# Issuing the one-hot sums of the expert keys one step behind their operands, loading stored activations and gates earlier, and pacing a gather's rest in a two-block transformer kernel

## The chip, the cores and the metric

The kernel runs on one core of one Trainium2 chip. The metric is the device time of one execution in microseconds (us). The core has five engines with instruction streams of their own: PE (TensorE, the matrix products), DVE (VectorE), ACT (ScalarE), POOL (GpSimd) and SP (SyncE, which here only issues transfers). 16 DMA engines do the transfers of all of them.

## The reference, cut to what matters

Two transformer blocks on 512 tokens of width 1024, in float32. The first has a convolution, sliding-window attention and a feed-forward part; the second has a gated mixing part, attention over selected keys, and, as its last part, a mixture of 16384 tiny experts, each a row of `u_tab` and a row of `v_tab`. The change lies in that last part alone:

```python
def peer(xn, wq, subkeys, u_tab, v_tab):
    q = (xn @ wq).reshape(bsz, s, PEER_HEADS, 2, PEER_HALF)
    sub = jnp.einsum('bshpd,hpnd->bshpn', q, subkeys)
    s_top, i_top = lax.top_k(sub, PEER_TOPK)
    cand = (s_top[..., 0, :, None] + s_top[..., 1, None, :]).reshape(...)
    cand_idx = (i_top[..., 0, :, None] * N_KEYS + i_top[..., 1, None, :]).reshape(...)
    best, pos = lax.top_k(cand, PEER_TOPK)
    expert = jnp.take_along_axis(cand_idx, pos, axis=-1)
    gate = jax.nn.softmax(best, axis=-1)
    ...
        a = jax.nn.gelu(jnp.einsum('td,ted->te', xb, u_tab[eb]))
        return jnp.einsum('te,ted->td', (gb * a).astype(vb.dtype), v_tab[eb])
```

Each token has 8 heads, 128 keys a half and 16 experts a head: 128 experts a token.

## The kernel before, in words

Products are made in float32 from a high and a low half of each factor, three matmuls for one (`mm3`, L155 to L158). Weights stream through `unit` (L132 to L141) in pieces of 128x1024, 512 KB: SP issues the load of `raw` (L134, four buffers), ACT rounds it to `whi` (L138), DVE subtracts for `wlo` (L140, four buffers each), PE uses both. PE can so be served up to four units ahead of what it computes, and DVE's `wlo` is the step that sets how far.

The expert part takes two ways. Tokens 0 to 319 go through **all** experts as dense products: activations of 320 tokens with every row of `u_tab`, times a gate matrix G that is zero but for the chosen experts, times `v_tab`. Tokens 320 to 511 (half a block of 128 and the whole last block) fetch their experts' rows from memory instead: `gathered` (L950 to L968) lets POOL fetch 128 rows a time (L944, seven buffers `rows`), and DVE multiplies and adds them: 64 times for the half block (L952), 128 times for the last block with `u_tab` (L960), 128 times with `v_tab` (L967).

**The u stage** (about 1040 to 1470 us of the profile): 128 units of `u_tab`, of which 100 are computed here (`u_block`, L932 to L940, 24 matmuls 128x320 each), and their results are stored in memory (`a_dram`, 640 KB for four units). After each, the loop at L1189 to L1197 hands a budget of `R_US` = 3.6 us to a generator, `routed`, whose `yield`s say what they cost of it; a second generator, `gathered`, gets a share of it. What a generator issues before its budget is gone stands in the program behind that u-block. `routed` (L1150 and on) makes the gates for the blocks of 128 tokens in the order tb 2, 3, 0, 1:

- `keys` finds the 16 best sums, and then turns the positions of the best into key numbers in four steps (two halves of the pair, eight of 16 places each): DVE compares (L1033) and multiplies by a copy of the numbers (L1034) into `ohl` (two buffers), and PE adds up over the eight places by matmuls with a unit matrix (L1037, for tb 2 L1039 too). Then the gates are normalised and transposed on PE (L1067).
- `build` makes G of a block of tokens in 16 half-steps: DVE makes one-hot tiles `oh1`, `oh2` (L1097, L1098) and weighted ones `ohh`, `ohl` (L1104), PE multiplies them (L1111, 16 matmuls 128x128), ACT copies the sums out (L1112), and a whole step goes to memory (`g_dram`, L1117). The last eight half-steps of tb 2, the last of all, use three weighted tiles (`ohm` too, of which there is one buffer): five DVE instructions and 24 matmuls.
- Before those, the rest of the half block's gather is run off in one go (`while not made2: next(gat)`), and `weights2` turns its sums into gates.

**The v stage** (about 1470 to 2106 us): for each pair of units, `first` has the stored activations `al` of four units loaded (L1214, two buffers) or computes the pair's activations, `second` has the gates `gl` of eight units loaded (L1228, 1536 KB, two buffers) and multiplies them on DVE (L1231); the result is split (ACT `wvhi` L152, DVE `wvlo` L153), and two `v_block`s use it, 18 matmuls 128x512 each. 28 u-blocks that were not stored lie between. The gather for the last block runs beside it, a share for each v-block. SP issues its loads in the order of the program: an `al` whose buffer is not free yet holds up the `raw`s behind it.

A scheduler sets the order of DVE, ACT and SP instructions within what the program's order allows; the gather's DVE instructions are tied to stand behind the newest `wlo`.

## Time and profile before

| | us |
|---|---|
| runs | 2113.63, 2115.81, 2117.98 (median 2115.81) |
| profiled execution: its time, its span | 2110.99, 2109.3 |
| PE busy | 2050.9 (97%), 11120 matmuls |
| DVE busy | 1573.4 (75%) |
| ACT busy | 826.6 (39%) |
| POOL busy | 527.7 (25%) |
| mean granted TensorE clock | 0.992 of 2.4 GHz |

The span goes from the first instruction to the last one. The share of busy time is taken over the whole program; how PE and DVE stand to each other differs from stage to stage, so the rows below are mostly of single stretches. A line is that of the kernel before; the same instruction has a higher line number in the changed one (L1037 becomes L1030, L1104 becomes L1119, L1214 becomes L1225, L1228 becomes L1235, L1231 becomes L1259).

### The profile page before, as it was taken

What the parts mean: (1) busy time and instruction counts of PE and PEld (TensorE: products, weight loads), DVE (VectorE), ACT (ScalarE), POOL (GpSimd) and SP (SyncE); (2) the same over time, 40 slices, a digit from 0 to 9 for tenths busy, and PEclk for the clock granted to TensorE, in tenths of its full rate; (3) what the DMA queues carried; (4) which work ended last, traced back from release to release, by engine and by line L of the source; (5) the groups of instructions that cost most, each with busy time, mean ns of one, the idle gap of its engine ahead of it and who ended that gap; (6) DMA issues with size and microseconds to landing.
All of it is one profiled execution on the core that took longest, in us unless ns stands there. A gap on an engine that the chain in (4) does not pass through costs nothing.

```text
span 2109.3 us, 29516 instructions
## 1 busy us (share of the span) xinstructions
PE 2050.9 (97%) x11120; PEld 1747.3 (83%) x11120; DVE 1573.4 (75%) x2885; ACT 826.6 (39%) x1339; POOL 527.7 (25%) x383
## 2 busy tenths in 40 slices
PE   7999999999999999999989999999999999999999
PEld 6747888888887777888889899999888878788887
DVE  6984633332279954455699999998898888899997
ACT  5364432231254242333453455555333333233332
POOL 1000100000010000000032212220676666566673
PEclk9999999999999999999999999999999999999999
DMA  5202233333223212342288899999999999999996
GB/s 190 80 30 80 85 96 100 99 92 119 81 86 94 82 59 81 109 135 86 90 305 268 290 316 335 309 369 294 397 404 412 387 408 388 410 400 410 411 400 248
DMA packets 163281, 476.47 MB, mean 226 GB/s; under 512 B 13865, under 2 KB 57265, under 8 KB 161218
## 3 DMA queue, kind: packets, MB, share of 16 engines
q1 hardware_dynamic: 67104, 259.70, 35.1%
q0 software_dynamic: 46656, 169.18, 21.0%
q10 hardware_dynamic: 49378, 45.71, 6.5%
q8 instruction: 87, 1.43, 0.3%
q14 instruction: 56, 0.46, 0.1%
HBM read 432.18 MB, written 42.09 MB: 225 GB/s over the span
## 4 chain that ended last, share of the span: by engine, by line
PE 62%; DVE 17%; issue 12%; DMA 5%; POOL 2%; ACT 2%; DVEq 0%; POOLq 0%; SPq 0%; ACTq 0%; another core or an unknown queue 0%
PE bank_a L156 14%; PE bank_a L157 14%; PE bank_a L158 14%; PE bank_b L156 5%; PE bank_b L157 5%; PE bank_b L158 5%; DVE wlo L140 4%; DMA rows<-in_peer_u_dram,gidx 2%; DMA al<-a_dram 2%; POOL rows L944 2%; DVE rows L952 2%; DVE rows L960 2%; PE bank_b L1111 1%; DVE mask L710 1%; DMA rows<-in_peer_v_dram,gidx 1%
## 5 line engine op out<-in xcount | busy, mean ns | idle before, releaser
L138 ACT CAST whi<-raw 128x1024 fp32r<-128x1024 f32 (+1 forms) x413 | 431.9, 1047 | 879.1 <-PE bank_a L157 336.2
L140 DVE TENSOR_TENSOR wlo<-raw,whi 128x1024 fp32r<-128x1024 f32 (+1 forms) x413 | 499.9, 1213 | 264.1 <-ACT whi L138 261.7
L156 PE MATMUL bank_a<-xhi,whi 128*128 128x320 f32 (+2 forms) x1600 | 550.0, 345 | 0.8 <-ACT xhi L152 0.8
L158 PE MATMUL bank_a<-xhi,wlo 128*128 128x320 f32 (+2 forms) x1600 | 545.5, 341 | 3.7 <-DVE wlo L140 3.7
L157 PE MATMUL bank_a<-xlo,whi 128*128 128x320 f32 (+2 forms) x1600 | 546.7, 342 | 0.6 <-DVE xlo L153 0.6
L944 POOL DMA_INDIRECT rows<-in_peer_u_dram,gidx x192 | 284.1, 1480 | 546.3 <-DVE gidx L1045 144.4
L158 PEld LDWEIGHTS bank_a<-xhi,wlo 128*128 128x128 f32 x1600 | 302.9, 189 | 31.5 <-DVE wlo L140 5.7
L156 PEld LDWEIGHTS bank_a<-xhi,whi 128*128 128x128 f32 x1600 | 302.1, 189 | 29.3 <-issue 2.3
L157 PEld LDWEIGHTS bank_a<-xlo,whi 128*128 128x128 f32 x1600 | 303.0, 189 | 27.4 <-DVE xlo L153 1.6
L944 POOL DMA_INDIRECT rows<-in_peer_v_dram,gidx x128 | 207.1, 1618 | 114.6 <-DVE h L967 89.9
L156 PE MATMUL bank_a<-whi,wvhi 128*128 128x512 f32 x512 | 201.6, 394 | 6.4 <-ACT wvhi L152 6.4
L158 PE MATMUL bank_a<-whi,wvlo 128*128 128x512 f32 x512 | 200.8, 392 | 1.5 <-DVE wvlo L153 1.5
L157 PE MATMUL bank_a<-wlo,wvhi 128*128 128x512 f32 x512 | 201.4, 393 | 0.6 <-DVE wlo L140 0.6
L967 DVE SCALAR_TENSOR_TENSOR h<-rows,ga,h 128x1024 f32<-128x1024 f32 x128 | 164.2, 1282 | 5.9 <-DMA rows<-in_peer_v_dram,gidx 4.6
L173 POOL TENSOR_TENSOR rstd<-rstd,neghalf 128x1 f32<-128x1 f32 x20 | 13.9, 695 | 616.2 <-DVE rstd L172 616.2
L960 DVE SCALAR_TENSOR_TENSOR rows<-rows,h 128x1024 f32<-128x1024 f32 x128 | 152.6, 1217 | 8.1 <-DMA rows<-in_peer_u_dram,gidx 8.1
L156 PEld LDWEIGHTS bank_a<-whi,wvhi 128*128 128x128 f32 x512 | 96.8, 189 | 27.1 <-ACT wvhi L152 7.6
L158 PEld LDWEIGHTS bank_a<-whi,wvlo 128*128 128x128 f32 x512 | 96.9, 189 | 24.5 <-DVE wvlo L153 3.9
L157 PEld LDWEIGHTS bank_a<-wlo,wvhi 128*128 128x128 f32 x512 | 96.9, 189 | 20.5 <-DVE wlo L140 1.4
L157 PE MATMUL bank_b<-wlo,wvhi 128*128 128x512 f32 x256 | 99.6, 389 | 0.0
L156 PE MATMUL bank_b<-whi,wvhi 128*128 128x512 f32 x256 | 99.6, 389 | 0.0
L158 PE MATMUL bank_b<-whi,wvlo 128*128 128x512 f32 x256 | 99.6, 389 | 0.0
(405 smaller groups left out, 3281.5 us busy)
## 6 DMA issues: line engine op xcount, KB each, us to landing
raw<-in_wt_dram SPq DMA_DIRECT2D x150, 512.0 KB
raw<-in_ut_dram SPq DMA_DIRECT2D x128, 512.0 KB
raw<-in_peer_v_dram SPq DMA_DIRECT2D x128, 512.0 KB
g_dram<-gt ACTq DMA_DIRECT2D x24, 896.0 KB
gl<-g_dram SPq DMA_DIRECT2D x14, 1536.0 KB
a_dram<-ab ACTq DMA_DIRECT2D x25, 640.0 KB
al<-a_dram SPq DMA_DIRECT2D x25, 640.0 KB
rows<-in_peer_u_dram,gidx POOLq DMA_INDIRECT x192
```

What stands on the lines that cost most here:

```text
L138: lead[0] = S.copy(hi[:, :n], raw[:, :n]).ins
L140: pace[0] = V.tensor_tensor(lo[:, :n], raw[:, :n], hi[:, :n].bitcast(F32), op=OP.subtract).ins
L156: T.matmul(o, lh, rh, start=start, stop=False)
L157: T.matmul(o, lh, rl, start=False, stop=False)
L158: T.matmul(o, ll, rh, start=False, stop=stop)
L173: rooted[0] = G.tensor_tensor(r, r, neghalf[:, 0:1], op=OP.pow).ins
L710: V.match_replace(out=sc, in_to_replace=m8, in_values=sc, imm_value=-3.3e38)
L944: G.indirect_dma_start(out=r, out_offset=None, in_=table, in_offset=bass.IndirectOffsetOnAxis(ap=idx[:, k:k + 1], axis=0))
L952: V.scalar_tensor_tensor(r, r, 1.0, hn2, op0=OP.mult, op1=OP.mult, accum_out=ga2[:, k:k + 1])
L960: V.scalar_tensor_tensor(r, r, 1.0, hn3, op0=OP.mult, op1=OP.mult, accum_out=ga[:, k:k + 1])
L967: V.scalar_tensor_tensor(h[3], r, ga[:, k:k + 1], h[3], op0=OP.mult, op1=OP.add)
L1111: T.matmul(gp[:, j, :], o_[:, g2, :, t2], oh1[:, g2, :, t2], start=o_ is ohs[0], stop=o_ is ohs[-1])
```

## The change

In `keys`, the four steps' matmuls are put in a function `sums` and issued one step after their operands; the gate's exponential moves ahead of the last sums, and the yields around are made smaller. In `routed`, the gather's rest is no longer run off in one go: each of its steps is charged to the budget, and `weights2` yields between its parts. In the v stage `al` has three buffers and is loaded one tile (four units) ahead; `gl` is loaded in two halves of 12 of its 24 slices, issued four and two units before its first use, and no longer at it.

```diff
--- before.py
+++ after.py
@@ -1023,6 +1023,15 @@
         V.tensor_copy(kf, ki_)
         pt = bank("b")
         pt2 = bank("b") if tb == 2 else None
+
+        def sums(a, b0, e3):
+            for b in range(8):
+                l, r = (ident16, e3[:, b]) if tb == 3 else (e3[:, b], ident16)
+                T.matmul(pt[:, a * 128:(a + 1) * 128], l, r, start=(b0 + b == 0), stop=(b0 + b == 15))
+                if tb == 2:
+                    T.matmul(pt2[:, a * 128:(a + 1) * 128], turn16, e3[:, b], start=(b0 + b == 0), stop=(b0 + b == 15))
+
+        late = None
         for a in range(2):
             for b0 in range(0, 16, 8):
                 sx = pr.tile([128, 4, 128, 2], F16, name="ohh", bufs=2).rearrange("p x i t -> p (x i t)")
@@ -1032,12 +1041,20 @@
                 e3 = eq.rearrange("p (b s) -> p b s", b=8)
                 V.tensor_tensor(e3, iotab[:, b0:b0 + 8], kf[:, a, None, :].to_broadcast([128, 8, 128]), op=OP.is_equal)
                 V.tensor_tensor(eq, eq, sx, op=OP.mult)
-                for b in range(8):
-                    l, r = (ident16, e3[:, b]) if tb == 3 else (e3[:, b], ident16)
-                    T.matmul(pt[:, a * 128:(a + 1) * 128], l, r, start=(b0 + b == 0), stop=(b0 + b == 15))
-                    if tb == 2:
-                        T.matmul(pt2[:, a * 128:(a + 1) * 128], turn16, e3[:, b], start=(b0 + b == 0), stop=(b0 + b == 15))
+
+                if late:
+                    sums(*late)
+                late = (a, b0, e3)
                 yield 1.4
+        ge = pr.tile([128, 8, 16], F32, name="ge")
+        V.tensor_tensor(ge, bv, bv[:, :, 0:1].to_broadcast([128, 8, 16]), op=OP.subtract)
+        S.activation(ge, ge, AF.Exp)
+        yield 0.7
+        sums(*late)
+        yield 0.3
+        gsu = small.tile([128, 8], F32, name="gsu")
+        V.tensor_reduce(gsu, ge, axis=AX.X, op=OP.add)
+        V.reciprocal(gsu, gsu)
         if tb == 2:
             S.copy(sl, pt2[:, 0:256].rearrange("p (a s) -> p a s", a=2))
             for p0 in (0, 64):
@@ -1045,12 +1062,6 @@
                 V.scalar_tensor_tensor(gidx2[p0:p0 + 64], sl[p0:p0 + 64, 0, s0:s0 + 64], 128.0, sl[p0:p0 + 64, 1, s0:s0 + 64],
                                        op0=OP.mult, op1=OP.add)
             ready.append(True)
-        ge = pr.tile([128, 8, 16], F32, name="ge")
-        V.tensor_tensor(ge, bv, bv[:, :, 0:1].to_broadcast([128, 8, 16]), op=OP.subtract)
-        S.activation(ge, ge, AF.Exp)
-        gsu = small.tile([128, 8], F32, name="gsu")
-        V.tensor_reduce(gsu, ge, axis=AX.X, op=OP.add)
-        V.reciprocal(gsu, gsu)
         if tb == 3:
             V.tensor_tensor(ggate.rearrange("p (h k) -> p h k", k=16), ge, gsu[:, :, None].to_broadcast([128, 8, 16]), op=OP.mult)
             S.copy(sl, pt[:, 0:256].rearrange("p (a s) -> p a s", a=2))
@@ -1063,19 +1074,23 @@
         g16 = kf[:, 0]
         V.tensor_copy(g16, sl[:, 0])
         V.tensor_tensor(sl[:, 1], sl[:, 0], g16, op=OP.subtract)
+        yield 1.0
         for j in range(2):
             T.transpose(pt[:, 256 + j * 128:384 + j * 128], sl[:, j], ident)
         S.copy(sTs[tb], pt.rearrange("p (a t) -> p a t", a=4))
         if tb == 2:
             S.activation(gT2, pt[:, 320:384], AF.Copy, scale=2.0 ** -14)
-        yield 3.0
+        yield 1.0
 
     def weights2():
 
+        yield 0.3
         S.activation(zg[64:128, 0:64], ga2[64:128], AF.Gelu_apprx_tanh)
         S.activation(zg[0:64, 64:128], ga2[0:64], AF.Gelu_apprx_tanh)
+        yield 0.7
         zp = bank("b")[:, 0:64]
         T.matmul(zp, zg, fold, start=True, stop=True)
+        yield 0.7
         V.tensor_tensor(gT2, zp, gT2, op=OP.mult)
         for j in range(3):
             V.tensor_copy(w2s[:, j], gT2)
@@ -1163,9 +1178,8 @@
                 yield from keys(pr, tb)
                 yield from build(pr, tb)
             while not made2:
-                next(gat)
-            weights2()
-            yield 0.5
+                yield next(gat)
+            yield from weights2()
             yield from build(pr, 2)
 
         keyed = []
@@ -1204,15 +1218,30 @@
         yb_ = [[bank("a") for _ in range(2)] for _ in range(2)] + [[bank("b") for _ in range(2)]]
         state = {"debt": 0.0}
 
+        def load_a(m):
+
+            if m < len(SPAIR) // 2:
+                state["a", m] = pv.tile([128, 4, N_U], F32, name="al", bufs=3)
+                nc.sync.dma_start(state["a", m], a_dram[m])
+
+        def load_g(g, k):
+
+            if g < N_RES:
+                state["g", g] = gres[g]
+            elif g < 16:
+                if k == 0:
+                    state["g", g] = pv.tile([128, 24, 8, 16], F32, name="gl", bufs=2)
+                sl = slice(12 * k, 12 * k + 12)
+                nc.sync.dma_start(state["g", g][:, sl], g_dram[g - N_RES][:, sl])
+
         def first(p, j):
 
             if j == 0:
                 if p in SPAIR:
                     n = SPAIR.index(p)
                     if n % 2 == 0:
-                        state["al"] = pv.tile([128, 4, N_U], F32, name="al", bufs=2)
-                        nc.sync.dma_start(state["al"], a_dram[n // 2])
-                    state[p] = state["al"][:, 2 * (n % 2):2 * (n % 2) + 2, :]
+                        load_a(n // 2 + 1)
+                    state[p] = state["a", n // 2][:, 2 * (n % 2):2 * (n % 2) + 2, :]
                 else:
                     state[p] = pv.tile([128, 2, N_U], F32, name="av", bufs=2)
             if p not in SPAIR:
@@ -1221,11 +1250,10 @@
         def second(p):
 
             i1 = 2 * p
-            if i1 % 8 == 0 and i1 // 8 < N_RES:
-                state["gl"] = gres[i1 // 8]
-            elif i1 % 8 == 0:
-                state["gl"] = pv.tile([128, 24, 8, 16], F32, name="gl", bufs=2)
-                nc.sync.dma_start(state["gl"], g_dram[i1 // 8 - N_RES])
+            if i1 % 8 == 0:
+                state["gl"] = state.pop(("g", i1 // 8))
+            elif i1 % 8 >= 4:
+                load_g(i1 // 8 + 1, i1 % 8 // 2 - 2)
             av = state.pop(p)
             g4 = state["gl"][:, :, i1 % 8:i1 % 8 + 2, :]
             V.tensor_tensor(g4[:, 0:N_U // 16], av.rearrange("p b (s t) -> p s b t", t=16), g4[:, 0:N_U // 16], op=OP.mult)
@@ -1241,6 +1269,8 @@
                     mm3(yb_[tb][hf], w[0][:, i1 % 2, tb * 128:(tb + 1) * 128], w[1][:, i1 % 2, tb * 128:(tb + 1) * 128],
                         vu[0][:, hf * 512:(hf + 1) * 512], vu[1][:, hf * 512:(hf + 1) * 512], i1 == 0, i1 == 127)
 
+        load_g(0, 0)
+        load_a(0)
         for j in range(2):
             first(0, j)
         w = second(0)
```

Where it moves instructions: three places, each first as it stood and then as it stands. A row is an instruction of the engine in its order (line, operation, output<-inputs, shape; "x2" is two alike in a row). Units are counted from the first one of the u stage as 1.

On DVE, around the sums of `keys` for tb 1, before. The two `wlo` rows are those of units 69 and 70; PE's first sums of this key stand behind 4 of the 24 matmuls of unit 68:

```order
L140 TENSOR_TENSOR wlo<-raw,whi 128x1024
L1033 TENSOR_TENSOR ohl<-iotab,kf 128x1024 x2
L1034 TENSOR_TENSOR ohl<-ohl,ohh 128x1024 x2
L1062 TENSOR_TENSOR slot<-ge,gsu 128x128
L1033 TENSOR_TENSOR ohl<-iotab,kf 128x1024
L1064 CAST kf<-slot 128x128
L1033 TENSOR_TENSOR ohl<-iotab,kf 128x1024
L1034 TENSOR_TENSOR ohl<-ohl,ohh 128x1024
L1065 TENSOR_TENSOR slot<-slot,kf 128x128
L1034 TENSOR_TENSOR ohl<-ohl,ohh 128x1024
L140 TENSOR_TENSOR wlo<-raw,whi 128x1024
```

And now, where the `wlo` rows are again those of units 69 and 70, and PE's first sums stand behind the whole of unit 68, its second ones behind unit 69:

```order
L1042 TENSOR_TENSOR ohl<-iotab,kf 128x1024 x2
L1043 TENSOR_TENSOR ohl<-ohl,ohh 128x1024 x2
L140 TENSOR_TENSOR wlo<-raw,whi 128x1024
L1056 TENSOR_REDUCE gsu<-ge 128x8
L1057 RECIPROCAL gsu<-gsu 128x8
L1072 TENSOR_SCALAR gsu<-gsu 128x8
L1073 TENSOR_TENSOR slot<-ge,gsu 128x128
L1075 CAST kf<-slot 128x128
L1076 TENSOR_TENSOR slot<-slot,kf 128x128
L140 TENSOR_TENSOR wlo<-raw,whi 128x1024
L1042 TENSOR_TENSOR ohl<-iotab,kf 128x1024 x2
L1043 TENSOR_TENSOR ohl<-ohl,ohh 128x1024 x2
```

The first two operand tiles moved ahead of the `wlo` of unit 69, the other two behind that of unit 70, and the gate's arithmetic stands between them. For the other blocks the same count gives: tb 2's first two steps of sums stand behind unit 8 in both kernels, its other two behind unit 9 now (behind 14 matmuls of unit 9 and behind unit 9 before). For tb 3 sums and operands both moved back, the sums from 7 matmuls into unit 16 to 14 matmuls into it, the operands by one `wlo`; for tb 0 likewise, from 8 matmuls into unit 44 to 3 into unit 45, and one `wlo`.

On DVE, at the end of the u stage, before: the last half-steps of `build`. The first `wlo` row is that of unit 102, the last one holds those of units 103 and 104 (`oh_13429` is `oh1` of the last half-step):

```order
L1104 TENSOR_TENSOR ohl<-oh_13391,w2s 128x1024
L140 TENSOR_TENSOR wlo<-raw,whi 128x1024
L1104 TENSOR_TENSOR ohm<-oh_13391,w2s 128x1024
L1097 TENSOR_TENSOR oh_13429<-iota_7110,sT_7093 128x1024
L1098 TENSOR_TENSOR oh_13430<-iota_7110,sT_7093 128x1024
L1104 TENSOR_TENSOR ohh<-oh_13430,w2s 128x1024
L1104 TENSOR_TENSOR ohl<-oh_13430,w2s 128x1024
L1104 TENSOR_TENSOR ohm<-oh_13430,w2s 128x1024
L140 TENSOR_TENSOR wlo<-raw,whi 128x1024 x2
```

And now, where the last row is the `wlo` of unit 104, and that of unit 103 stands a half-step ahead of the first row:

```order
L1119 TENSOR_TENSOR ohm<-oh_13350,w2s 128x1024
L1112 TENSOR_TENSOR oh_13391<-iota_7110,sT_7093 128x1024
L1113 TENSOR_TENSOR oh_13392<-iota_7110,sT_7093 128x1024
L1119 TENSOR_TENSOR ohh<-oh_13392,w2s 128x1024
L1119 TENSOR_TENSOR ohl<-oh_13392,w2s 128x1024
L1119 TENSOR_TENSOR ohm<-oh_13392,w2s 128x1024
L1112 TENSOR_TENSOR oh_13429<-iota_7110,sT_7093 128x1024
L1113 TENSOR_TENSOR oh_13430<-iota_7110,sT_7093 128x1024
L1119 TENSOR_TENSOR ohh<-oh_13430,w2s 128x1024
L1119 TENSOR_TENSOR ohl<-oh_13430,w2s 128x1024
L1119 TENSOR_TENSOR ohm<-oh_13430,w2s 128x1024
L140 TENSOR_TENSOR wlo<-raw,whi 128x1024
```

Of tb 2's half-steps, three more stand behind the last stored u-block, unit 100. On PE, two half-steps (48 matmuls of L1111) stood between units 100 and 101, and now five (120) do, while ahead of unit 100 there are 72 fewer. DVE's instructions up to the v stage are the same in kind and number.

On SP, around a group of gates in the v stage, before (`raw` rows are the weight loads of units):

```order
L1264 DMA h_70<-h_dram 128x1024
L134 DMA raw<-in_peer_v_dram 128x1024
L1228 DMA gl<-g_dram 128x3072
L134 DMA raw<-in_peer_v_dram 128x1024 x3
L1214 DMA al<-a_dram 128x1280
L134 DMA raw<-in_ut_dram 128x1024
L134 DMA raw<-in_peer_v_dram 128x1024
L134 DMA raw<-in_ut_dram 128x1024
L134 DMA raw<-in_peer_v_dram 128x1024
```

And now, the same stretch:

```order
L1294 DMA h_70<-h_dram 128x1024
L134 DMA raw<-in_peer_v_dram 128x1024
L1235 DMA gl<-g_dram 128x1536
L134 DMA raw<-in_peer_v_dram 128x1024
L1235 DMA gl<-g_dram 128x1536
L134 DMA raw<-in_peer_v_dram 128x1024 x2
L1225 DMA al<-a_dram 128x1280
L134 DMA raw<-in_ut_dram 128x1024
L134 DMA raw<-in_peer_v_dram 128x1024
L134 DMA raw<-in_ut_dram 128x1024
L134 DMA raw<-in_peer_v_dram 128x1024
```

The load of the gates became two with a `raw` between them. The `al` row stands where it stood, but is now the tile that DVE uses one `al` later. A `raw` can be issued when the `wlo` four units before it has freed its buffer; so counted on SP and DVE together, seven of the 25 `al` loads before were issued three units or fewer ahead of their first use (two of them one unit); now one is (three units), and the others stand 5 to 24 units ahead. Of the 14 gate loads, all stood three units or more ahead; now the first half has the place of the whole, and the second half stands 0 to 2 `raw`s behind it, which for five of them is two units or one ahead of the use.

## Rows read from the trace of the kernel before

**Rows 1.** Waits of PE, u stage, 1040 to 1500 us: total us, times, longest us.

```profile
PE bank_b L1037 <- DVE ohl L1034: 9.3, 4, 2.6
PE bank_a L158 <- DVE wlo L140: 3.7, 7, 0.9
PE bank_b L1111 <- DVE ohh L1104: 1.1, 1, 1.1
...
PE bank_b L156 <- ACT gt L1112: 0.3, 1, 0.3
```

**Rows 2.** Waits of PE, v stage, 1500 to 2109 us.

```profile
PE bank_a L156 <- ACT wvhi L152: 6.4, 3, 3.7
PE bank_a L158 <- DVE wvlo L153: 1.5, 3, 0.7
PE bank_a L157 <- DVE wlo L140: 0.6, 1, 0.6
```

**Rows 3.** Timeline of PE: start us, us, instruction, [idle before <-releaser].

```profile
1096.78 0.61 PE L1037 MATMUL bank_b<-ohl,ident 128*128 128x128 f16 x8 [2.26 <-DVE ohl L1034]
...
1205.12 0.82 PE L1037 MATMUL bank_b<-ident,ohl 128*128 128x128 f16 x8 [2.02 <-DVE ohl L1034]
...
1311.45 1.03 PE L1037 MATMUL bank_b<-ident,ohl 128*128 128x128 f16 x8 [2.43 <-DVE ohl L1034]
...
1412.40 0.29 PE L1111 MATMUL bank_b<-oh,ohh 128*128 128x128 f16 x2 [1.11 <-DVE ohh L1104]
...
1845.60 0.50 PE L156 MATMUL bank_a<-whi,wvhi 128*128 128x512 f32 x1 [3.65 <-ACT wvhi L152]
```

**Rows 4.** Windows: us; busy of PE, PEld, DVE, ACT, POOL; granted clock, DMA share, GB/s.

```profile
1097.00:1098.00 1.00, 1.00 (x17) 0.94 (x15) 1.00 (x3) 0.99 (x2) 0.00 (x0) 1.00 1.04 422
1220.00:1300.00 80.00, 80.00 (x685) 78.24 (x684) 80.00 (x169) 47.09 (x86) 16.89 (x14) 1.00 1.00 334
1310.00:1330.00 20.00, 18.55 (x145) 17.95 (x146) 17.19 (x29) 7.91 (x12) 3.77 (x3) 0.91 0.68 245
1720.00:1740.00 20.00, 16.91 (x73) 13.35 (x72) 18.23 (x27) 7.01 (x10) 11.94 (x8) 0.91 1.02 401
1840.00:1860.00 20.00, 15.94 (x62) 12.39 (x61) 19.89 (x19) 7.04 (x8) 13.43 (x10) 0.91 1.00 382
1900.00:1940.00 40.00, 40.00 (x187) 33.67 (x186) 38.21 (x36) 13.09 (x14) 26.91 (x16) 1.00 1.02 411
2080.00:2100.00 20.00, 20.00 (x89) 16.54 (x89) 14.20 (x13) 3.90 (x4) 0.94 (x1) 1.00 0.40 154
```

**Rows 5.** Timeline of DVE, last half-steps of the u stage (columns as in group 3).

```profile
1462.18 0.68 DVE L1104 TENSOR_TENSOR ohm<-oh,w2s 128x1024 bf16<-128x1024 f16 x1
1462.78 0.69 DVE L1097 TENSOR_TENSOR oh<-iota,sT 128x1024 f16<-128x1024 f16 x1
...
1466.47 0.69 DVE L1104 TENSOR_TENSOR ohm<-oh,w2s 128x1024 bf16<-128x1024 f16 x1 [1.07 <-PE bank_b L1111]
```

**Rows 6.** Waits of DVE, v stage, 1500 to 2109 us.

```profile
DVE gl L1231 <- DMA al<-a_dram: 19.6, 5, 5.0
DVE rows L960 <- DMA rows<-in_peer_u_dram,gidx: 8.1, 9, 2.2
...
DVE gl L1231 <- DMA gl<-g_dram: 4.9, 3, 3.0
```

**Rows 7.** Timeline of SP, then DVE: an al load's issue, and the use it holds up.

```profile
1651.35 0.33 SPq L1214 DMA_DIRECT2D al<-a_dram  x1
...
1660.18 0.82 DVE L1231 TENSOR_TENSOR gl<-al,gl 128x640 f32<-128x640 f32 x1 [3.96 <-DMA al<-a_dram]
...
1822.68 0.33 SPq L1214 DMA_DIRECT2D al<-a_dram  x1
...
1834.58 0.83 DVE L1231 TENSOR_TENSOR gl<-al,gl 128x640 f32<-128x640 f32 x1 [4.06 <-DMA al<-a_dram]
```

**Rows 8.** Waits of SP's own queue, v stage.

```profile
SPq L134 <- DVE wlo L140: 449.4, 140, 8.4
```

## The prediction

> **What bounds the kernel now.** I read first the table of busy times (PE 97%), so the time is PE's work plus its idle time; then PE's waits, apart for the two stages that the change touches; then the timeline around the longest waits; and last, per stage, what the engine that PE waits for was itself waiting for. PE's waits are short and few. In the u stage they sum to about 15 us: 9.3 in the sums of `keys`, one for each of the four blocks (2.6, 2.26, 2.02 and 2.43), 3.7 for `wlo`, 1.1 in `build`, and little else [rows 1, 3]. In the v stage there are 8.5 us (6.4 + 1.5 + 0.6), of which the longest is 3.65 [rows 2, 3].
>
> A long wait costs more than itself. In the 20 us around the tb 1 wait, and around each of the two long ones of the v stage, the mean granted clock is 0.91; elsewhere it stands at 1.00 [rows 4]. The lower of the clock's two levels (1.2 and 2.4 GHz) is a half, so 0.09 x 20 / 0.5 = 3.6 us ran at it, in which 1.8 us of work was not done. The wait of 2.26 us at 1096 had no such tail (17 short matmuls in the microsecond behind it, clock 1.00), so 2 us of idle time is about where it can go either way.
>
> In the u stage DVE is the engine without slack: between 1220 and 1300 it was busy 80.00 of 80 us, PE too [rows 4]. What is taken from PE's waits there counts only if DVE doesn't arrive later for it. In the v stage DVE is ahead of PE except where a load was late: 19.6 us of waiting for `al` in five waits, 4.9 for `gl` in three [rows 6]. The issue of such an `al` to its use took 8.8 us (1651.35 to 1660.18) and 11.9 us (1822.68 to 1834.58) [rows 7], and it was issued late since its buffer was late, not since the transfer was long. SP itself mostly waits for free weight buffers (449 us of `raw` behind `wlo`), not for the memory [rows 8].
>
> **The change part by part.** The same instructions run but for the split `gl` loads (14 more DMA issues on SP), so all of the change is in waits.
>
> *Sums a step behind their operands.* The wait of a sum is DVE being late, so what counts is how far PE's place and DVE's place moved against each other. For tb 1 DVE's first two operand tiles now stand one `wlo` earlier and PE's sums 20 matmuls later. I count that wait as gone with its clock tail: 2.43 + 1.8 = 4.2 us. (The second pair of tiles is due one unit later on both, so it should be just in time; if it isn't, see the rivals.) For tb 3 and tb 0 both sides moved back alike, one `wlo` against 7 and 19 matmuls, so 2.26 and 2.02 stay; for tb 2 the place of the first sums hasn't moved, so 2.6 stays. These three count nothing, though the text of the change touches all four.
>
> *The gather's rest in turn.* In a burst DVE put its row multiplies ahead of the tiles that PE wanted; the wait of 1.11 us in `build` at 1412.40 [rows 3] is what came of it. Gone: 1.1 us.
>
> The price: charged to the budget, that rest pushes `build` back, and three half-steps of tb 2 now stand behind unit 100, where no u-block lies between them. A half-step is five DVE instructions 0.60 us apart (1462.18 to 1462.78) [rows 5], 3.0 us, and 24 PE matmuls, at 17 in a microsecond [rows 4] 1.4 us. `ohm` has one buffer, so DVE's next `ohm` waits for PE, as at 1466.47 (1.07) [rows 5]. With DVE as far ahead as that buffer lets it, PE ends the first of the five half-steps 1.4 us after unit 100, the second's `ohm` is ready 0.6 later, the third's, fourth's and fifth's 3.0 us apart behind it (5.0, 8.0, 11.0), and PE is through 1.4 us later: 12.4 us, for 5 x 1.4 = 7.0 us of work. So 5.4 us of idle time stand where there were 0.3 [rows 1]: 5.1 us lost. That PE's total of half-steps is the same doesn't help, since ahead of unit 100 it has fewer to do and hurries to the same DVE. Whether the clock falls is open: each gap is about 1.6 us, between the 1.11 after which it didn't and the 2.02 to 2.43 after which it mostly did, but four of them come in a row. I take one tail, 1.8 us; the bounds are 0 and twice that.
>
> The u stage by itself: 4.2 + 1.1 - 5.1 - 1.8 = **1.6 us lost** (bounds: 0.2 gained without the clock's tail, 7.6 lost with two tails and tb 1's wait kept).
>
> *`al` in three buffers, a tile ahead.* The lead of the late ones was one to three units, now it is five and more but for one. A unit of the v stage takes 18 matmuls at 89 in 20 us [rows 4], 4.0 us; five units are 20 us against a landing of 8.8 to 11.9 [rows 7]. All 19.6 us of DVE's waits for `al` should go. The third buffer takes 5 KB a partition and no instruction.
>
> *`gl` in halves.* Five second halves are issued two units or fewer ahead of use: 8.1 us. No row shows a half landing. An `al` of 640 KB took 8.8 to 11.9 us, so 768 KB would take 10.6 to 14.3 by size; from below, nothing is waited for if a half lands within 8.1. I take 10.6, the unhurried end, since the whole `gl` of 1536 KB, issued three units ahead (12 us), was waited for but three times, 4.9 us in all [rows 6]. That makes five waits of 2.5 us, 12.5 on DVE. What PE sees of it: 8.5 us for 19.6 + 4.9 = 24.5 on DVE, 0.35 of each; so 4.4 us of PE's idle time come back or stay.
>
> The v stage: 8.5 - 4.4 = 4.1 us of waits and both clock tails, 3.6: **7.7 us gained** (bounds: 12.1 if no `gl` is late, 0 if the transfers set the pace).
>
> **Sum**: 7.7 - 1.6 = 6.1 us less. The profiled execution took 2110.99 us and the runs' median was 2115.81, 4.8 above; the sum applies to either, and against the median it gives **2109.7 us**. Runs of the kernel before differ by 4.4 us, so 0.2% (4.2 us: below 2111.6, above 2120.0) is about what can be told from no change.
>
> **The rivals.**
>
> 1. *The transfers bound the v stage.* From 1900 to 1940 the DMA engines are busy at a share of 1.02, 411 GB/s, and only in the last stretch (154 GB/s from 2080) is there room [rows 4]. An earlier `al` then only makes something else late, the gather's rows first: DVE waited 8.1 us for those already [rows 6]. Against: there was room between 1310 and 1330 (245), PE ran 40.00 of 40 us at 411 GB/s without a wait, and SP waits for buffers [rows 4, 8]. The v stage would gain nothing: 2115.8 + 1.6 = **2117.4**, no change. The Trainium skill speaks for this one: "DMA: Bandwidth & Descriptors", in its section on issuing engines not being separate DMA queues, says that transfers of all engines end up on the same 16 DMA engines and interleave there. By that rule an early load takes the others' bandwidth while they are full; whether it costs here depends on who has slack, and no row shows that yet.
> 2. *Slower: the gates' second halves.* If a half lands 14.3 us after its issue, the upper end above, the five with two units' lead wait 6.2 each and three with three units' lead (12.1) 2.2 each: 38 us on DVE, at 0.35 some 13.1 on PE, with two tails as now. The v stage then loses 13.1 - 8.5 = 4.6, with the u stage's 1.6 that is **2122.0**. It decides from a landing of some 12 us on. For it: the halves are issued into a full memory queue, and behind a `raw`. Against: smaller than the whole, which was waited for little.
> 3. *tb 1's wait stays*, since the second operands stand behind one `wlo` more: 4.2 us of the gain are gone, **2113.9**, no change. DVE's lack of slack speaks for it, PE's 20 matmuls against it.
> 4. *All of it goes*: the sums' waits of the other three blocks too (2.6 + 2.26 + 2.02, and two tails, 3.6), as the name of the change promises, the tail of half-steps without a clock fall, no late `gl`: 4.2 + 1.1 + 10.5 - 5.1 + 12.1 = 22.8, **2093.0**. Against it speaks the order of the instructions, in which these places didn't part.
>
> **How the numbers follow.** Forecast 0.50, by itself 2103.5 (gain 12.1 + 0.2) to 2114 (a gain of 2, between those bounds' lower sides); the transfers 0.18; the gates slower 0.14; tb 1's wait 0.10; all of it 0.08. Faster: 0.43 of the forecast's and rival 4's 0.08, with some of rival 3, 0.54. Slower: rival 2 and a little of rival 1's upper side, 0.15. The same: 0.31. Both signs hold weight, so the range has to reach into the transfers and part of the gates: 2102 to 2121 leaves out rival 4 and the worse half of rival 2, 0.15 or so.
>
> **What would show it.** In the changed profile: PE's waits in the sums at three, not four, with about 7 us; none in the first wait of `build`, but some 5 us for `ohm` just ahead of the v stage, and a clock below 1 there; no DVE wait for `al`; a few for `gl`, about 2.5 us each, with PE's v-stage waits near 4 us. I am wrong if waits for `al` are replaced by waits for rows (rival 1), if `gl` waits pass 30 us (rival 2), or if the half-steps behind unit 100 run without gaps, which would mean that DVE was further ahead than the single `ohm` allows.

## The result

The change made the kernel slower: 2131.42 us (median of 7 runs, 2123.24 to 2134.56) against 2114.39 us before (7 runs, 2111.03 to 2117.98), a ratio of 1.0071 with a 95% interval of 1.0057 to 1.0085. Forecast were 2109.7 us and at most 2121.0. The profiled execution took 2128.54 us, its span is 2126.8.

To see where the 17.5 us between the two spans lie, each profile is cut at two points that PE's timeline shows in both: its first wait for `wlo` in the u stage (1052.94 us before, 1055.72 now) and the end of the last one-hot matmul (1468.58, 1477.19). Up to the first point the code is the same; the 2.8 us there come of a lower clock between 113 and 125 us (first row of the windows below). The profiles of the runs further down, with the same code up to there, differ in it too: the mean granted clock of these 12 us is 1.00 in the kernel before, 0.86 in three runs and 0.54 to 0.72 in all others. The u stage grew from 415.6 to 421.5 us (+5.8), the v stage up to the last matmul from 636.8 to 645.6 (+8.8). Forecast were +1.6 and -7.7.

PE's waits in the u stage now (1040 to 1500 us; total us, times, longest us), to be set beside [rows 1]:

```profile
PE bank_b L1030 <- DVE ohl L1043: 11.6, 4, 4.2
PE bank_a L158 <- DVE wlo L140: 3.6, 6, 1.1
PE bank_b L1126 <- DVE ohm L1119: 2.1, 4, 1.2
PE bank_b L1126 <- DVE ohh L1119: 2.1, 4, 0.6
...
PE bank_b L1126 <- DVE ohl L1119: 1.0, 3, 0.4
```

The sums still have four waits, with 11.6 us in place of 9.3, and `build` has 5.2 us for its three weighted tiles in place of 1.1. Three of the four in the timeline, for tb 3, tb 0 and tb 1 (where [rows 3] had 2.26, 2.02 and 2.43), and then the first of the half-steps behind unit 100:

```profile
1101.59 0.86 PE L1030 MATMUL bank_b<-ohl,ident 128*128 128x128 f16 x8 [4.16 <-DVE ohl L1043]
...
1213.75 0.62 PE L1030 MATMUL bank_b<-ident,ohl 128*128 128x128 f16 x8 [3.25 <-DVE ohl L1043]
...
1323.83 1.22 PE L1030 MATMUL bank_b<-ident,ohl 128*128 128x128 f16 x16 [1.64 <-DVE ohl L1043]
...
1466.46 0.23 PE L1126 MATMUL bank_b<-oh,ohm 128*128 128x128 f16 x1 [1.24 <-DVE ohm L1119]
1468.39 0.29 PE L1126 MATMUL bank_b<-oh,ohh 128*128 128x128 f16 x2 [0.61 <-DVE ohh L1119]
1469.00 0.29 PE L1126 MATMUL bank_b<-oh,ohl 128*128 128x128 f16 x2 [0.32 <-DVE ohl L1119]
```

Windows of the changed kernel (columns as in [rows 4]); the third number from the right is the granted clock:

```profile
113.00:125.00 12.00, 11.56 (x36) 4.74 (x38) 5.86 (x9) 5.24 (x10) 0.00 (x0) 0.72 0.14 44
1060.00:1080.00 20.00, 16.29 (x150) 15.69 (x149) 19.94 (x82) 11.86 (x17) 3.67 (x4) 1.00 0.65 209
1100.00:1120.00 20.00, 18.41 (x134) 18.10 (x134) 18.76 (x68) 8.87 (x13) 2.71 (x4) 0.91 0.82 273
1460.00:1480.00 20.00, 15.07 (x165) 13.27 (x164) 15.05 (x23) 9.32 (x20) 0.00 (x0) 1.00 0.78 256
```

The clock stayed up through the whole row of half-steps (1460 to 1480: 1.00, with 4.9 us idle) and fell behind tb 3's wait of 4.16 us (1100 to 1120: 0.91).

In the v stage, PE's waits (1500 us to the end), beside [rows 2], and DVE's, beside [rows 6]:

```profile
PE bank_a L156 <- ACT wvhi L152: 8.8, 3, 3.1
PE bank_a L157 <- DVE wlo L140: 4.7, 4, 2.1
PE bank_a L158 <- DVE wvlo L153: 1.6, 4, 0.5
```

Together PE waits 15.1 us here, where 8.5 stood before and 4.4 were forecast.

```profile
DVE gl L1259 <- DMA gl<-g_dram: 28.3, 7, 10.3
...
DVE wlo L140 <- ACT whi L138: 7.7, 7, 3.1
DVE gres L1259 <- ACT av L940: 7.6, 2, 5.3
DVE rows L960 <- DMA rows<-in_peer_u_dram,gidx: 4.8, 6, 1.4
```

The waits for `al`, 19.6 us, are gone to the last; those for `gl` grew from 4.9 to 28.3 us. DVE's waits for `av` grew from one of 3.2 us to two of 7.6. The longer one, 5.3 us, has this behind it: at the stage's start five `al` and four halves of `gl` are issued within 25 us, and the weights issued behind them, at 1514.18, were ready for ACT at 1530.13. The longest wait for `gl` in the timelines of SP and of DVE, with a pair of halves ahead of it that were issued one behind the other ("x2"):

```profile
1959.51 0.80 SPq L1235 DMA_DIRECT2D gl<-g_dram  x2
...
1981.72 0.33 SPq L1225 DMA_DIRECT2D al<-a_dram  x1
1983.79 0.33 SPq L1235 DMA_DIRECT2D gl<-g_dram  x1
1986.12 1.47 SPq L134 DMA_DIRECT2D raw<-in_peer_v_dram  x2
1987.64 0.43 SPq L1235 DMA_DIRECT2D gl<-g_dram  x1
...
1971.56 0.82 DVE L1259 TENSOR_TENSOR gl<-al,gl 128x640 f32<-128x640 f32 x1 [0.93 <-DMA gl<-g_dram]
...
2001.76 0.82 DVE L1259 TENSOR_TENSOR gl<-al,gl 128x640 f32<-128x640 f32 x1 [10.27 <-DMA gl<-g_dram]
```

The close pair was usable 12.1 us after its issue; the pair with two weight loads between it 18.0 us after the first half's and 14.1 after the second's. Of these 18.0 us, 3.9 passed before the second half was issued at all: the weight loads between the halves first wait on SP for a free buffer, 2.6 us of waits for `wlo` between 1982 and 1990.

### The profile page after: what moved, and what is told of

It is laid out like the page before. It is cut to its first block, busy times and chain, and to the rows that moved or that the text cites. A ratio compares the mean times of both kernels' runs of the same rounds, so it can differ in the third digit from the quotient of the medians.

```text
span 2126.8 us, 29552 instructions
## 1 busy us (share of the span) xinstructions
PE 2056.4 (97%) x11120; PEld 1748.6 (82%) x11120; DVE 1573.9 (74%) x2885; ACT 826.0 (39%) x1339; POOL 528.1 (25%) x383
## 5 line engine op out<-in xcount | busy, mean ns | idle before, releaser
L158 PEld LDWEIGHTS bank_a<-whi,wvlo 128*128 128x128 f32 x512 | 97.2, 190 | 23.9 <-DVE wvlo L153 3.3
```

The lines of the kernel that those rows point to most:

```text
L158: T.matmul(o, ll, rh, start=False, stop=stop)
```

## The experiments

Below, *u* and *v* are the lengths of the two stages in a run's own profile, cut as above. The change has four parts: K (`keys`), G (the gather's rest in turn), A (`al`), L (`gl` in halves).

| kernel | median us | ratio to before (95%) | profiled execution, us | u | v |
|---|---|---|---|---|---|
| before | 2114.4 to 2116.2 | 1 | 2111.0 | 415.6 | 636.8 |
| the change: K, G, A, L | 2131.42 | 1.0057 to 1.0085 | 2128.5 | 421.5 | 645.6 |
| v_only: A, L | 2123.41 | 1.0023 to 1.0056 | 2124.6 | 415.1 | 648.0 |
| u_only: K, G | 2121.96 | 1.0014 to 1.0048 | 2127.7 | 421.8 | 642.5 |
| al_only: A | 2113.16 | 0.9978 to 1.0003 | 2113.8 | 415.9 | 634.9 |
| gl_only: L | 2123.93 | 1.0029 to 1.0072 | 2130.2 | 415.8 | 651.7 |
| k_only: K | 2121.30 | 1.0010 to 1.0047 | 2125.9 | 418.5 | 645.7 |
| g_only: G | 2127.96 | 1.0047 to 1.0089 | 2131.3 | 419.8 | 647.9 |
| gl_adj | 2130.27 | 1.0056 to 1.0099 | 2131.4 | 421.4 | 646.7 |
| gl_whole: K, G, A | 2117.29 | 0.9992 to 1.0013 | 2118.9 | 421.6 | 633.5 |
| tail | 2124.62 | 1.0024 to 1.0053 | 2121.7 | 416.3 | 646.9 |
| after_half | 2105.95 | 0.9940 to 0.9973 | 2105.5 | 421.5 | 622.8 |
| before_half | 2100.44 | 0.9900 to 0.9939 | 2100.8 | 415.6 | 622.4 |
| al_pair | 2113.60 | 0.9972 to 1.0000 | 2115.1 | 414.7 | 637.1 |
| al_225 | 2105.91 | 0.9927 to 0.9966 | 2107.8 | 415.8 | 629.3 |
| al_220 | 2107.04 | 0.9946 to 0.9974 | 2107.0 | 417.7 | 626.6 |
| after_220 | 2130.68 | 1.0054 to 1.0094 | 2125.8 | 419.0 | 644.4 |

A profile is one execution, and it lies up to 6.3 us off its kernel's median. The eight profiles with the old u stage give 414.7 to 417.7 us for it, the six with the new one 419.0 to 421.8. No kernel's v stage was profiled twice, so a difference of a few us between two v stages is shown only where the medians show it too. Behind PE's last matmul 3.8 to 4.0 us are left in all profiles but those of al_220 and after_220, where it is 7.8 and 7.9.

**The parts by themselves.** The first four runs put parts of the change on the kernel before. *v_only* is its v stage with the old u stage, *u_only* the reverse; *al_only* and *gl_only* have one v-stage part, by these lines of the change and the old ones for the other:

```diff
+ (al_only)  state["a", m] = pv.tile([128, 4, N_U], F32, name="al", bufs=3)
+ (gl_only)  elif i1 % 8 >= 4: load_g(i1 // 8 + 1, i1 % 8 // 2 - 2)
```

> The kernel before with the v stage of the change alone (al a tile ahead in three buffers, gl in halves). Theory Q: SP's loads share one queue, so a load lands as late as what was issued ahead of it; the gates' second halves, issued behind two more raw loads, and the bunch of early loads at the start of the v stage cost 5 to 11 us whatever the u stage does: 2119 to 2126 against 2114.4 before, with DVE waits for gl of 20 us or more. Rival S: the v stage only suffers because the u stage now ends in a row of half-steps and hands over late; then this gains as forecast, 2104 to 2110.

> The kernel before with the u stage of the change alone (sums a step late, gather's rest in turn), its v stage as before. Theory Q: 4 to 7 us slower (2118 to 2122), all of it lost before the v stage: some 5.2 us of idle time for ohm behind unit 100 and longer waits in the sums of tb 3 and tb 0. Rival S: 12 to 16 us slower (2126 to 2130), since the late handover costs the v stage too.

> The kernel before with al alone in three buffers and a tile ahead; gl whole, as before. Theory Q: DVE's 19.6 us of waits for al go, PE's v-stage waits of 8.5 us fall below 3, less up to 3 us for one more load in the bunch at the start: 2104 to 2111. Rival S: an early al holds SP up at its buffer and crowds the raw loads: 2116 to 2124.

> The kernel before with gl alone in halves, issued four and two units ahead; al as before, in two buffers. Theory Q: al's waits stay and those for gl come on top: 5 to 12 us slower, 2119 to 2126, with a second half landing some 14 us after its issue. Rival S: the halves are no slower than the whole: 2112 to 2117.

Measured: v_only is 7.3 us slower than before (2123.41 against 2116.12 on the same chip), with 28.6 us of DVE waits for `gl`; gl_only 7.8. So the gates' halves cost what theory Q said, and need no help of the u stage. DVE's waits in gl_only's v stage show both late loads side by side:

```profile
DVE gl L1240 <- DMA gl<-g_dram: 24.4, 5, 11.1
DVE gl L1240 <- DMA al<-a_dram: 18.6, 5, 5.9
```

u_only is 5.8 us slower in the median, within theory Q's 4 to 7 and below rival S's 12 to 16. Its u stage grew as the change's did, by 6.2 us, so the median leaves nothing for the v stage. In the profile the v stage, whose code is the old one, is longer too (642.5), but that execution lies 5.8 us above its median. What is different there for certain is the order of the loads, which the scheduler set anew, and DVE's waits for `al`, 25.0 us where they were 19.6. Counted on SP and DVE, the fifth `al` stood three units ahead of its use before and stands one unit ahead here, and DVE waits for it, at a place where it had no wait before:

```profile
1569.22 1.56 DVE L1245 TENSOR_TENSOR gl<-al,gl 128x640 f32<-128x640 f32 x2 [5.54 <-DMA al<-a_dram]
```

al_only misses by size: its waits for `al` fall from 19.6 to 1.6 us, but the v stage is only 1.9 us shorter, and PE waits 7.3 us where it waited 8.5:

```profile
PE bank_a L156 <- ACT wvhi L152: 5.5, 3, 2.0
PE bank_a L158 <- DVE wvlo L153: 1.8, 4, 0.5
```

The memory's rate from 1500 to 2060 us, the last number of these windows, first before and then in al_only, left no room to move them into:

```profile
1500.00:2060.00 560.00, 551.54 (x2588) 465.26 (x2588) 515.48 (x591) 195.35 (x220) 364.52 (x225) 0.99 1.02 403
```

```profile
1500.00:2060.00 560.00, 552.79 (x2603) 467.55 (x2602) 519.83 (x596) 194.95 (x221) 362.41 (x225) 0.99 1.02 407
```

The DMA engines are busy at a share of 1.02 in both; whether they or the memory behind them are what is full is not told apart here, and "the memory" below stands for either. So the waits have moved to other loads, which DVE's waits in al_only show: those for `whi`, which ACT makes of the weights, were 3.0 us before, and those for `gl` grew from 4.9 to 7.8.

```profile
DVE wlo L140 <- ACT whi L138: 11.2, 9, 2.6
...
DVE gl L1236 <- DMA al<-a_dram: 1.6, 1, 1.6
```

Rival S's hold-up of SP has at most a small part: from 1500 to 2060 us SP stood 22.8 us at an `al` whose buffer DVE had yet to free before, and 26.6 in al_only. One place, in the timelines of SP, ACT and DVE: three `al` are issued between the weight loads, the weights of that stretch come late, ACT stands for them, and the activations `av` that DVE wants are queued on ACT behind such a weight.

```profile
1706.77 0.43 SPq L1211 DMA_DIRECT2D al<-a_dram  x1
...
1712.16 0.33 SPq L1211 DMA_DIRECT2D al<-a_dram  x1
...
1717.06 0.33 SPq L1211 DMA_DIRECT2D al<-a_dram  x1
...
1733.46 1.05 ACT L138 CAST whi<-raw 128x1024 fp32r<-128x1024 f32 x1 [4.63 <-DMA raw<-in_peer_v_dram]
1734.42 0.43 ACT L940 ACTIVATE av<-bank_b 128x320 f32<-128x320 f32 x1
...
1734.88 0.82 DVE L1236 TENSOR_TENSOR gl<-av,gl 128x640 f32<-128x640 f32 x1 [1.35 <-ACT av L940]
```

**K and G apart, and the halves' neighbours.** *k_only* and *g_only* are the kernel before with the new `keys`, and with these lines:

```diff
             while not made2:
-                next(gat)
-            weights2()
-            yield 0.5
+                yield next(gat)
+            yield from weights2()
```

> The kernel before with the new keys alone (sums a step late, gate arithmetic ahead of the last ones). Theory Q: tb 1's wait and its clock tail shrink, tb 3's and tb 0's grow, as in the profile of the change; by that the sum is about nothing: 2113 to 2119 against 2116. Rival T (the row of half-steps behind unit 100 comes from keys' smaller yields, not from the gather's rest): 4 to 6 us slower, with some 5 us of waits for ohm ahead of the v stage.

> The kernel before with the gather's rest in turn alone. Theory Q: the burst's wait of 1.1 us goes, and some 5 us of idle time stand behind unit 100: 3 to 6 us slower, 2119 to 2122. Rival T: no row of half-steps, so a gain of about 1 us.

Both u stages grew, by 2.8 and 4.2 us; K alone leaves three half-steps behind unit 100 and G alone four, so rival T is right about K and theory Q about G, and neither about both: each pushes `build` back. Both v stages, again old code, are 9 to 11 us longer in profiles that lie 3 to 5 us above their medians, with 23.9 and 33.2 us of waits for `al`. By the medians, 5.1 and 11.8 us slower, the u stages leave 2.3 and 7.5 us for the rest. That G alone costs more than K and G together isn't a sum of parts: the order of the v stage's loads falls out differently each time, which fits it and is not shown to be the whole cause.

*gl_adj* issues both halves at one place:

```diff
-            elif i1 % 8 >= 4:
-                load_g(i1 // 8 + 1, i1 % 8 // 2 - 2)
+            elif i1 % 8 == 4:
+                load_g(i1 // 8 + 1, 0)
+                load_g(i1 // 8 + 1, 1)
```

> The changed kernel with both halves of the gates issued at the first one's place, four units ahead, one behind the other. Theory Q (the loss is the weight loads that stand between the halves): the second half lands as the whole did, 10 to 11 us behind the first one's issue; DVE's waits for gl fall from 28 us to under 12, and the time by 3 to 6 us, 2124 to 2128 against 2131. Rival H (two transfers of 12 slices are slower than one of 24): waits stay above 20 us and the time within 2 us of the change's.

This one did not make its edit: the weight loads between the halves are earlier in the program, and the scheduler left them there in 9 of the 14 groups, with waits of 25.6 us. As a whole it decides nothing between Q and H. One late group was mended, though, the eighth. In the change and then in gl_adj, from the timelines of SP and DVE:

```profile
1793.49 0.33 SPq L1235 DMA_DIRECT2D gl<-g_dram  x1
1795.82 0.33 SPq L134 DMA_DIRECT2D raw<-in_peer_v_dram  x1
1796.20 0.42 SPq L1235 DMA_DIRECT2D gl<-g_dram  x1
...
1808.84 0.83 DVE L1259 TENSOR_TENSOR gl<-al,gl 128x640 f32<-128x640 f32 x1 [5.13 <-DMA gl<-g_dram]
```

```profile
1797.58 0.80 SPq L1235 DMA_DIRECT2D gl<-g_dram  x2
...
1810.39 0.82 DVE L1260 TENSOR_TENSOR gl<-al,gl 128x640 f32<-128x640 f32 x1 [2.59 <-DMA gl<-g_dram]
```

From the first half's issue to the use it took 15.4 us with the weight load between the halves and 12.8 without, and from the second half's 12.6 and about 12.4. So here the gap costs what it delays the second half's issue by, 2.7 us, which is theory Q's side; the whole gates of this group took 11.2 us in gl_whole (below), so up to 1.6 us can be the cut's own.

**The memory's rate.** *after_half*, and later *before_half*, leave out every second row fetch of the gather:

```diff
-            r = gather(A["peer_u"], gidx, k)
+            r = gather(A["peer_u"], gidx, k) if k % 2 == 0 else r
```

> The changed kernel with every second row fetch of the last block's gather left out (DVE uses the row tile of the fetch before once more, in place of the one it should have): a quarter of the v stage's bytes less, DVE's work the same. Theory Q, sharpened (the memory's rate, 410 GB/s in every window, is what the loads wait for): DVE's waits for gl fall below 8 us and PE's v-stage waits below 4, 9 to 14 us less than the change. Rival P (the loads are issued too late, whatever the rate): waits for gl stay above 15 us, time within 5 us of the change's.

> The kernel before with every second row fetch of the last block's gather left out (DVE uses the tile of the fetch before once more). Theory M: the late al loads land in 5 us or less, PE's v-stage waits go below 1 us and the v stage takes 623 us, as it does in the change with the same fetches left out, 14 us less than before: 2100 to 2104. Rival P (al is late since it is issued late, whatever the rate): five waits of 1 us or more for al stay, with 4 us or more of PE waits, 2106 to 2112.

Both v stages take 622 to 623 us and PE waits in neither; after_half is 25 us below the change, more than expected. Its window reads 304 GB/s at a DMA share of 0.86:

```profile
1500.00:2060.00 560.00, 560.00 (x2659) 476.17 (x2659) 527.93 (x606) 198.99 (x225) 186.17 (x115) 1.00 0.86 304
```

DVE's waits there, of after_half and then of before_half:

```profile
DVE wlo L140 <- ACT whi L138: 20.1, 16, 2.9
DVE gl L1259 <- DMA gl<-g_dram: 10.9, 5, 5.5
```

```profile
DVE gl L1231 <- DMA al<-a_dram: 8.1, 6, 1.9
```

Some waits stay, so rival P isn't quite wrong, but DVE then has the slack to hide them. So 14 us of the v stage before, and 23 of the change's, go with these fetches. The edit takes away more than bytes: POOL's work falls by half too, from 364.5 to 186.2 us in these 560 (the fifth busy time of the rows). Which of the two counts is not told apart by it; that it is the memory is argued.

*gl_whole* is the change with the gates loaded whole, at the first half's place; *tail* charges the gather's rest less; *al_pair* loads `al` in smaller pieces.

```diff
(gl_whole)
+            elif i1 % 8 == 4:
+                load_g(i1 // 8 + 1)
(tail)
-                yield next(gat)
+                next(gat)
+                yield 0.3
(al_pair)
+                state["a", n] = pv.tile([128, 2, N_U], F32, name="al", bufs=6)
...
+                    load_a(n + 4)
```

> The changed kernel with the gates loaded whole again, issued at the place of the first half, four units ahead. Theory M (in the v stage the memory's rate sets the pace, and a gate load that is cut in two with weight loads between its parts lands later and holds the gather's DVE work up behind it): DVE's waits for gl fall from 28 us to 6 to 10, the v stage gets 8 to 11 us shorter, the time 2119 to 2124 against the change's 2131. Rival H (an earlier place in the program is what hurts, whole or half): within 3 us of the change.

> The changed kernel with each step of the gather's rest charged 0.3 us to the budget in place of 1.3; three half-steps now stand behind unit 100, not five. By the prediction's price of a half-step there (3.0 us on DVE, 1.4 on PE) the idle time for ohm and its two companions falls by 2 x 1.6 = 3.2 us, from 5.2 to about 2, and the u stage by as much. Rival: DVE arrives as late with two half-steps less, and the idle time only moves ahead of unit 100.

> The kernel before with the stored activations loaded by pairs of units (320 KB) in six buffers, four pairs ahead, in place of 640 KB in two; gl whole, as before. Theory M: no waits for al, and raw loads held up less than with 640 KB at a time, so a v stage of 628 to 635 us against 637: 2108 to 2114. Rival B (bytes alone count): the same as with three buffers, 635 us, 2113.

gl_whole takes 12.1 us off the change's v stage (645.6 to 633.5), a little more than expected, and 14.1 off its median; the place isn't what hurt. SP's waits at an `al` whose buffer was not free fall with it, from 39.7 to 25.7 us in the v stage: late gates had also held up the loads behind. The same stretch as above, in its timelines of SP and DVE:

```profile
1976.67 0.33 SPq L1225 DMA_DIRECT2D al<-a_dram  x1
1978.73 0.33 SPq L1233 DMA_DIRECT2D gl<-g_dram  x1
1981.06 1.47 SPq L134 DMA_DIRECT2D raw<-in_peer_v_dram  x2
...
1991.05 2.30 DVE L1257 TENSOR_TENSOR gl<-al,gl 128x640 f32<-128x640 f32 x3 [4.61 <-DMA gl<-g_dram]
```

The same two weight loads stand behind the whole here, not between its parts, and 12.3 us after the issue the gates are there, against 18.0.

tail: the waits for the three weighted tiles fall from 5.2 to 2.7 us (1.5 for `ohm`, 0.9 for `ohh`, 0.3 for `ohl`), where 2.0 was expected, and the u stage by 5.2. Of that, 2.5 us are those waits and 1.7 a clock fall less; 1 us I can't place. DVE does not arrive as late as before, so the rival is out.

al_pair has no wait for `al` and yet a v stage as before: rival B. Its median, 2113.60, is al_only's.

**Asking for less.** The last three keep all bytes and instructions of al_only, or of the change, and only slow the gather down (al_225 here):

```diff
-G_US = 2.3
+G_US = 2.25
```

> al alone in three buffers, a tile ahead, and the last block's gather given 2.25 us of a v-block's budget in place of 2.3: the same bytes and instructions, some five row fetches moved behind the last weights, where the memory is idle. Theory M (the v stage is paced by the memory's rate): the weight and gate loads get the 1% that the gather leaves, the v stage shrinks from 635 us by 2 to 6, 2107 to 2111. Rival N (bytes are not the bound; each wait has its own place): the same as with al alone, 2112 to 2115.

> The same with 2.2 us, some eleven row fetches moved behind the last weights. Theory M: the v stage shrinks by 3 to 8 us up to the last weights, but the eleven row products (1.3 us each, 14 us) just fill the last units' 17 us, so 0 to 3 us of that may be given back at the end: 2106 to 2112. Rival N: 2112 to 2118.

> The changed kernel with 2.2 us in place of 2.3 for the gather in a v-block. Theory M: DVE's waits for gl shrink from 28 us to 15 to 22 and the time by 3 to 8 us, 2123 to 2128. Rival N: waits of 26 us or more, within 2 us of 2131.

al_225 is 0.54% faster than before (0.34 to 0.73), al_220 0.40%; both beat the kernel before and the change. PE's longest v-stage wait in al_225, of 3.1 us in all:

```profile
PE bank_a L156 <- ACT wvhi L152: 2.8, 1, 2.8
```

al_220 gains more up to PE's last matmul (626.6), but gives 3.9 us back behind it (7.8 us to the end, where al_only has 3.9). Neither run is free of a rival: the pace also changes the order in which SP issues its loads, and how much of the gain that makes was not tried.

With the halves, in after_220, nothing comes of it: DVE's waits for `gl` are 33.0 us, as rival N had it. So two causes are left for the v stage: the full memory, which is why an earlier `al` brings next to nothing, and the torn gate loads, which land late whatever the gather asks for within this range. The second is shown by gl_only and gl_whole, the first argued from runs that all point to it.

## Why the prediction was wrong, point by point

- **gl in halves** is the step that failed most. I sized it at 10.6 us to land, by a half's bytes, and five DVE waits of 2.5 us. Measured were seven waits with 28.3 us. Sizing by bytes is what went wrong: a half took as long from its issue as the whole had. The second halves of the seven waits were usable 10.6 to 14.1 us after their issue, the whole gates of the kernel before 10.5 to 11.0 (its three waits). And six of these seven second halves were issued 1.5 to 3.9 us behind the first, since weight loads stand between (12.1 us from the first half's issue for a pair without any, 18.0 with two). That is rival 2's case (28 us on DVE, where it had 38); loading the gates whole takes 12.1 us off the v stage. What the cut itself costs apart from its neighbours is bounded by one group of gl_adj only, at up to 1.6 us, and stays open beyond it.
- **PE's share of DVE's waits**, taken as 0.35, isn't a constant: al_only has 9.4 us of DVE waits for `al` and `gl` and 7.3 on PE, the change 28.3 and 15.1.
- **al a tile ahead**: the waits for `al` went, as said, but I gave it all of PE's v-stage waits and clock tails, 12.1 us less what `gl` takes. By itself it gave 3 us in the median, not clear of nothing (0.9978 to 1.0003). This is rival 1, to which I gave 0.18: the memory was at its rate with it and without, and the weights are what waits instead. The Trainium skill ("DMA: Bandwidth & Descriptors", the section on issuing engines not being separate DMA queues) says that all transfers interleave on the same 16 engines; by that rule an early load delays others. The runs agree: half of the gather's rows less made the waits of PE vanish, a pace 2 or 4% lower gave 6 to 8 us up to PE's last matmul (al_only's v stage of 634.9 against 629.3 and 626.6, of which al_220 gives 3.9 back).
- **The row of half-steps** was right: 5.4 us of idle time priced, 4.9 measured (the 5.2 above less a wait of 0.28 at 1333), in four gaps. The clock tail of 1.8 us that I added did not come.
- **The sums**: tb 1's wait was to go and shrank to 1.64 us, without a clock tail. tb 3's and tb 0's, which I left unchanged since both sides moved alike, grew from 2.26 to 4.16 and from 2.02 to 3.25. One `wlo` of 1.2 us and what DVE does with it stand against 7 or 19 matmuls of 0.15 us; I called that alike. For tb 3 these are 1.2 against 1.05 us, for tb 0 1.2 against 2.85, by which tb 0's wait should have shrunk; why it grew stays open. tb 2's stayed at 2.55, as said.
- **The clock in the u stage**: I put one fall there, behind tb 1's wait, and 1.00 elsewhere. The kernel before has three, a mean of 0.91 from 1060 to 1080, from 1200 to 1220 and from 1310 to 1330. The changed one has two, behind the waits of tb 3 and tb 0. By 1.8 us each, the u stage's loss of 5.8 is 6.6 us more of waits (15.0 to 21.6) less one fall, and 1 us that stays open.
- **The burst** went: no wait at that place.
- **What I did not look at**: the u stage's change reorders the loads of the v stage, whose own code is the same in u_only, k_only and g_only. DVE's waits for `al` grew there from 19.6 to 23.9 to 33.2 us, and the profiled v stages by 6 to 11; by the medians about 0, 2 and 7 us of that are left. The order of these loads could have been counted for each part before.

## What to carry to other kernels

Where nearly every window of a stage shows the memory at one and the same rate, a wait for a late load is not won by loading earlier: something else is late then. Ask for less at that time, or move it to where the memory idles (here 2% less pace for a gather). And before a load is cut in two, look at how long loads of any size take there from issue to use, and at what the queue will hold between the parts.

## What was not expected of the hardware

The clock's fall behind a wait is not settled by the wait's length. The same wait of 2.55 us for tb 2's sums was followed by a mean clock of 1.00 from 1060 to 1080 in the change (window above); in the kernel before the same 20 us read 0.91, and in v_only, whose code is that of the kernel before up to there, 1.00 again, behind a wait of 2.54:

```profile
1060.00:1080.00 20.00, 16.91 (x144) 16.44 (x145) 19.09 (x80) 9.91 (x15) 5.36 (x5) 0.91 0.62 215
```

And 4.9 us of idle time in gaps of up to 1.24 us, within 10 us, brought no fall at all.
